# A planner that counts engine exclusion, and matmul operands at one place modulo 512 bytes, in a hybrid encoder block

## The chip, the cores and the metric

The kernel runs as one program on one core of a Trainium2 chip. The metric is device microseconds from a run of the program; before the change it is 2054.53 us, the median of three runs (2053.8 to 2062.17 us). Engines are named as in the profile: PE multiplies matrices (PEld is its weight load), DVE and POOL do elementwise work, ACT does activations and copies, SP issues DMAs.

## The reference

The block is one layer over a sequence of 1024 frames of width 1024, in float32. Two mixers run on the projected input and are gated and summed; then come an output projection and a convolutional feed-forward network, each with a residual and a layer norm.

```python
proj = h @ w_in                               # h: (1024, 1024), w_in: (1024, 7456)
u, v, rk, gates = split(proj)
y_a = gelu(u) * (blockwise w_s @ layer_norm(gelu(v)) + b_s)
rk = rk + (token_shift(rk) - rk) * mu_shift
r, k, val, wd, ad, gd = split(rk)
y_b = rwkv7(r, k, val, decay(wd), a(ad), gate(gd))   # 16 heads of 64, a recurrence over the frames
m = sigmoid(gate_a) * y_a + sigmoid(gate_b) * y_b
x = layer_norm(alpha * h + m @ w_o)
g, val = split(x @ w_up)                      # 2 x 2688 columns
x = layer_norm(alpha * x + (gelu(conv3(g)) * val) @ w_down)
```

## The kernel before, in words

Every large product is kept accurate in three passes: each operand is split into a high part rounded to fp32r and a low remainder, and `mm3` issues high by high, high by low and low by high into one PSUM bank. One such matmul has a 128x128 stationary operand and 512 moving columns. These "wide" matmuls are the bulk of PE's work.

The program has five stretches:

- Layer norm of the trunk input, transposition into `xh`/`xlo`, and the value projection `v` of the gating unit (tiles `vh`, `vl`, `pv`).
- The interleaved stretch. `load_w` fetches a 512 KB weight tile `wr` over SP, ACT rounds it to `wh`, POOL subtracts to get `wl`; `gemm` multiplies it with `xh`/`xlo` into `ps` (47 such tiles, 48 wide matmuls each). Beside that, 16 units (8 pairs of heads, two halves of the sequence) go through the recurrence: `stage_a` makes `ar`, `bk`, `nb`, `bkt`, `sv` on DVE, ACT and POOL and multiplies `bk` by `ar` into `pp`; `stage_b` solves a triangular system on POOL in 31 steps (`tm`, `yd`); `stage_chain` carries the state through eight chunks (`pc`, `py`, `xs`, `sv`), each chunk waiting for the one before; `stage_fin` finishes the unit.
- The output projection `po`, with `mh`/`ml` (tiles `wh`, `wl`) stationary and `woh`/`wol` moving, and the layer norm after it.
- The feed-forward network in seven groups of three column blocks: up projections `pu` and `ps` (stationary `fuh`/`ful` or `wh`/`wl`, moving `x1h`/`x1l`), convolution and gelu, and down projections `pd` (stationary `th`/`tl`, moving `fdh`/`fdl`), added into `acc` on DVE.
- The final layer norm (`finish`), row block by row block.

In the interleaved stretch the order on each engine is not the order of the Python code. The class `Weave` records every operation, gives it a cost by `cost` (L107 of the code before), links dependent operations, and then `order` (L209) simulates the five engines: it takes whichever engine can start first, and on it the ready operation with the lowest priority number. The order so found is then issued as it stands. PE, DVE, ACT and POOL each run their own list in that order, so an operation that waits holds up everything behind it on its engine. The planner's costs reach the chip only through this order. Outside the interleaved stretch the framework places the operations, and it lets the work of later code slip in between: the last projection weight (rows of L92) stands among the chunks of the last unit's chain.

`tiny` (L280) is a pool of small tiles that lies ahead of nearly everything else in on-chip memory; `gb` (L1043) is a buffer of the convolution, ahead of `t0`, `th` and `tl`.

Of the kernel before, what the change touches and what calls it, by code (L numbers as in the profile page):

```python
# [8 lines left out]
F32 = mybir.dt.float32  # L9
# [5 lines left out]
P = 128  # L15
D = 1024
S = 1024
# [33 lines left out]


class Op:
    __slots__ = ("key", "op", "call", "prio", "cost", "lat", "table", "deps", "users", "left", "ready", "seq", "out", "at", "cls", "wide")


class WovenPool:
# [17 lines left out]
class Weave:  # L75
# [14 lines left out]
    def add(self, key, op, fn, a, k):  # L90
        if not self.on:
            return fn(*a, **k)  # L92
        aps = [q for q in (*a, *k.values()) if isinstance(q, bass.AP)]
        o = Op()
        o.key, o.op, o.call, o.prio = key, op, (fn, a, k), self.prio
        if callable(o.prio):
            o.prio = o.prio(key)
        o.out, o.cls = aps[0], self.cls
        o.table = next((self.TABLE[q] for q in a if isinstance(q, AF) and q in self.TABLE), None) if key == "A" else None
        o.cost, o.lat = self.cost(key, op, aps, a)  # L100
        o.lat += self.late
        o.wide = key == "T" and aps[1].dtype == F32R and aps[0].shape[-1] == HT
        o.deps, o.users, o.seq = set(), [], len(self.ops)
        self.ops.append((o, aps[:1], aps[1:]))

    @staticmethod
    def cost(key, op, aps, a):  # L107
        n = int(np.prod(aps[0].shape[1:]))
        if op == "dma_start":
            return 60, 2000 + aps[0].size() * 4 / 150  # L110
        if key == "T":
            if aps[1].dtype == F32R:
                c = 233 * n / 512
            elif aps[1].shape[0] == 32:
                c = 50
            else:
                c = (1 if op == "transpose" else 2) * max(85 if n <= 64 else 111, 0.87 * n)
            return max(c, 30), 200
        if key == "A":
            return 150 + 0.95 * n, 80  # L120
        if key == "V":
            src = int(np.prod(aps[1].shape[1:])) if len(aps) > 1 else n
            k = max(n, src)
            if op in ("tensor_copy", "tensor_scalar", "tensor_scalar_max", "memset", "reciprocal"):
                return 150 + 0.8 * k, 80
            if op == "transpose":
                return 435, 80
            if op == "tensor_tensor_scan":
                return 190 + 1.7 * k, 80
            return 190 + (1.05 if k < 512 else 1.3) * k, 80  # L130
        if op == "memset":
            return 80 + 0.9 * n, 80
        return (200 + n if op == "tensor_copy" else 230 + 2.15 * n), 80

    @staticmethod
    def cells(ap):
# [71 lines left out]

    def order(self):  # L209
        free = dict.fromkeys("TVAGS", 0.0)  # L210
        held, small = {}, 0.0
        self.held = held
        table, todo = None, {k: [] for k in "TVAGS"}
        for o, _, _ in self.ops:
            o.left, o.ready = len(o.deps), 0.0
            if not o.left:
                todo[o.key].append(o)
        out = []
        while any(todo.values()):
            best = None  # L220
            for k, lst in todo.items():
                if lst:
                    t = max(free[k], min(self.start(o) for o in lst))
                    if best is None or t < best[0]:
                        best = t, k
            t, k = best
            can = [o for o in todo[k] if self.start(o) <= t]
            o = min(can, key=lambda o: (o.prio, o.seq))
            if k == "T":
                wide = [q for q in can if q.wide]  # L230
                if small > 900 and wide and o.cls != "stage_chain":
                    o = min(wide, key=lambda o: (o.prio, o.seq))
                small = 0.0 if o.wide else small + o.cost
            todo[k].remove(o)
            c = o.cost
            if k == "A" and o.table and (table or "-") not in o.table:
                table, c = o.table[0], c + 1283
            o.at = t
            free[k] = t + c
            for name in {ap.tensor.name for ap in self.aps[o.seq]}:  # L240
                if name in self.tag:
                    if name not in held:
                        held[name] = 0.0
                        self.lines[self.line[name]].pop(0)
                        self.next.remove(name)
                        self.room[self.tag[name]].remove(min(self.room[self.tag[name]]))
                    held[name] = max(held[name], t + c + 100)
                    self.uses[name] -= 1
                    if not self.uses[name]:
                        self.room[self.tag[name]].append(held[name])  # L250
            out.append(o)
            for u in o.users:
                u.left -= 1
                u.ready = max(u.ready, t + c + (o.lat if u.key != k or o.op == "dma_start" else 0))
                if not u.left:
                    todo[u.key].append(u)
        assert len(out) == len(self.ops)
        return out
# [13 lines left out]
def hybrid_block(ctx: ExitStack, tc, x, w_in, w_v, pars, rows, bs, ws, lor, w_o, w_up, w_dn, out):  # L272
# [4 lines left out]

    const = ctx.enter_context(tc.tile_pool(name="const", bufs=1))
    dram = ctx.enter_context(tc.tile_pool(name="dram", bufs=1, space=bass.MemoryType.DRAM))
    tiny = W.enter(ctx, tc.tile_pool(name="tiny", bufs=4), 4)  # L280

    v_d = dram.tile([KT, P, KT, P], F32, name="v_d")
    m_d = dram.tile([KT, P, S], F32, name="m_d")
# [710 lines left out]
    with ExitStack() as st:  # L994
# [40 lines left out]
        for g in range(NF // GRP):  # L1035
            hh, hl, wd = [], [], []
            for f in range(g * GRP, (g + 1) * GRP):
                wg = load2(w_up[f], "fu", 2) if f else wg0
                wv = load_w(0, w_up[NF + f]) if f else wv0
                wd.append(load2(w_dn[f * P:(f + 1) * P, :], "fd", GRP))  # L1040
                th = hp.tile([P, S], F32R, name="th")
                tl = hp.tile([P, S], F32R, name="tl")
                gb = fs.tile([P, S + 2], F32, name="gb", bufs=1)  # L1043
                G.memset(gb[:, 0:2], 0.0)
                cw = lambda i: par[:, C_CW + i * NF + f:C_CW + i * NF + f + 1]
                ts = []
                for h in range(2):
                    pg = up(wg, h, True) if f or h else up0[0]
                    A.copy(gb[:, 2 + h * HT:2 + (h + 1) * HT], pg)
                    t0 = fs.tile([P, HT], F32, name="t0", bufs=3)  # L1050
                    A.activation(t0, pg, AF.Identity, bias=par[:, C_CB + f:C_CB + f + 1], scale=cw(2))
                    V.scalar_tensor_tensor(t0, gb[:, 1 + h * HT:1 + (h + 1) * HT], cw(1), t0, ALU.mult, ALU.add)
                    V.scalar_tensor_tensor(t0, gb[:, h * HT:(h + 1) * HT], cw(0), t0, ALU.mult, ALU.add)
                    A.activation(t0, t0, AF.Gelu)
                    ts.append(t0)
                for h in range(2):
                    hs = slice(h * HT, (h + 1) * HT)
                    pv = up(wv, h) if f or h else up0[1]
                    V.tensor_tensor(ts[h], ts[h], pv, ALU.mult)
                    V.tensor_copy(th[:, hs], ts[h])  # L1060
                    G.tensor_tensor(tl[:, hs], ts[h], th[:, hs].bitcast(F32), ALU.subtract)
                hh.append(th)
                hl.append(tl)
            if g == 0:
                bc = load_bc(2)
                for i in range(2):
                    A.mul(bc[i], bc[i], ALPHA)
                for n in range(KT):
                    V.tensor_tensor(acc[n], acc[n], bc[0], ALU.mult)
                    (V if n % 2 else G).tensor_tensor(acc[n], acc[n], bc[1], ALU.add)  # L1070
            if g == NF // GRP - 1:
                bc = load_bc(4)
            for n in range(KT):
                ns = slice(n * P, (n + 1) * P)
                for j in range(2):
                    js = slice(j * HT, (j + 1) * HT)
                    po = ps_d.tile([P, HT], F32, name="pd")
                    for i in range(GRP):
                        mm3(po, hh[i][:, ns], hl[i][:, ns], wd[i][0][:, js], wd[i][1][:, js], i == 0, i == GRP - 1)
                    V.tensor_tensor(acc[n][:, js], acc[n][:, js], po, ALU.add)  # L1080
                if g == NF // GRP - 1:
                    finish(n, bc)
# [65 lines left out]
```

## Time and profile before

| | |
|---|---|
| runs | 2053.8, 2054.53, 2062.17 us |
| profiled execution: own time, span | 2061.35 us, 2059.6 us |
| mean granted PE clock in it | 0.954 of full speed |
| busy share of the span | PE 94%, PEld 75%, DVE 50%, POOL 44%, ACT 41% |
| stretches (us from the span's start) | first 0 to 110, interleaved 110 to 1204, output projection 1204 to 1397, feed-forward 1397 to 2026, end 2026 to 2059.6 |

A matmul's own duration in the profile overlaps its neighbours, so PE's pace is read from start to start, or from the chain of waits, where a row gives the time that a run of matmuls takes and their count. A row of waits names who waited for whom and how long in total. An idle engine costs nothing unless the chain goes through it. [...]

### The profile page before, as it was taken

How to read it: one execution, taken by the hardware profiler on the slowest of the kernel's cores; microseconds unless marked ns; L12 is line 12 of the kernel's file. 1: busy time of each engine (PE TensorE's matmuls, PEld its weight loads, DVE VectorE, ACT ScalarE, POOL GpSimd, SP SyncE). 2: the span in 40 equal slices, each digit the busy share in tenths (PEclk: the TensorE clock that was granted, in tenths of full speed). 3: DMA queues.
4: the chain of work that ended last, by engine and by line, in shares of the span. 5: the costliest groups of instructions: out<-in, count | busy, mean ns of one | idle time of the engine just before them, and what ended most of it. 6: DMA issues, size and time to landing. Idle time of an engine off the chain costs nothing.

```text
span 2059.6 us, 27150 instructions
## 1 busy us (share of the span) xinstructions
PE 1926.8 (94%) x10024; PEld 1541.6 (75%) x10024; DVE 1025.1 (50%) x1786; ACT 852.7 (41%) x1711; POOL 907.6 (44%) x1481
## 2 busy tenths in 40 slices
PE   6997998999999999999998876999999999999997
PEld 5995776667777777777776655877888888888886
DVE  8424545666666555565555257575232323232327
ACT  5443454565555656556654452331212121213121
POOL 5103463556667555556545336073414132323224
PEclk9998898999999999989987888999999999999999
DMA  5111211111111212111111050131112020211102
GB/s 202 45 36 55 56 50 54 50 47 50 47 50 61 63 50 67 41 50 49 53 52 39 25 202 27 39 123 61 62 31 71 22 72 23 70 32 60 42 0 82
DMA packets 76580, 119.13 MB, mean 58 GB/s; under 512 B 27520, under 2 KB 47232, under 8 KB 76448
## 3 DMA queue, kind: packets, MB, share of 16 engines
q1 hardware_dynamic: 59488, 96.94, 15.6%
q10 hardware_dynamic: 16960, 20.45, 3.0%
q8 instruction: 80, 1.31, 0.3%
q14 instruction: 52, 0.43, 0.1%
HBM read 103.08 MB, written 14.29 MB: 57 GB/s over the span
## 4 chain that ended last, share of the span: by engine, by line
PE 40%; DVE 5%; POOL 2%; issue 1%; DMA 1%; ACT 1%; SPq 0%; POOLq 0%; ACTq 0%; DVEq 0%
PE ps L92 11%; PE pd L92 10%; PE pu L92 10%; PE po L92 4%; DVE acc L92 3%; PE ps L267 2%; PE pp L267 2%; PE pc L267 1%; POOL yd L267 1%; POOL tm L267 1%; DVE ln_st L92 0%; PE pt L92 0%; DMA wor<-in_dram 0%; DVE t L92 0%; DVE wl L92 0%
## 5 line engine op out<-in xcount | busy, mean ns | idle before, releaser
L267 PE MATMUL ps<-xh,wh 128*128 128x512 f32 x752 | 323.0, 430 | 23.3 <-ACT wh L267 10.6
L267 PE MATMUL ps<-xh,wl 128*128 128x512 f32 x752 | 319.2, 425 | 4.5 <-POOL wl L267 4.4
L267 PE MATMUL ps<-xlo,wh 128*128 128x512 f32 x752 | 321.1, 427 | 0.0
L92 DVE SCALAR_TENSOR_TENSOR t<-gb,par,t 128x512 f32<-128x512 f32 x84 | 88.5, 1053 | 199.0 <-ACT t L92 197.6
L267 PEld LDWEIGHTS ps<-xh,wh 128*128 128x128 f32 x752 | 147.7, 197 | 51.7 <-ACT wh L267 10.8
L267 POOL TENSOR_TENSOR tm<-yd,da 128x60 f32<-128x60 f32 (+24 forms) x496 | 158.1, 319 | 54.2 <-ACT xs L267 8.7
L267 POOL TENSOR_TENSOR yd<-yd,tm 128x60 f32<-128x60 f32 (+24 forms) x496 | 163.6, 330 | 36.8 <-POOL tm L267 0.2
L267 PEld LDWEIGHTS ps<-xh,wl 128*128 128x128 f32 x752 | 147.3, 196 | 32.1 <-POOL wl L267 6.1
L267 DVE SCALAR_TENSOR_TENSOR sv<-pc,gam,sgm 64x64 f32<-64x64 f32 x240 | 68.0, 283 | 199.0 <-PE pc L267 197.0
L267 POOL TENSOR_TENSOR wl<-wr,wh 128x1024 fp32r<-128x1024 f32 x47 | 116.4, 2477 | 114.6 <-ACT wh L267 73.3
L267 PEld LDWEIGHTS ps<-xlo,wh 128*128 128x128 f32 x752 | 147.8, 197 | 25.0 <-issue 2.3
L92 DVE TENSOR_TENSOR acc<-acc,pd 128x512 f32<-128x512 f32 x112 | 76.8, 686 | 134.0 <-PE pd L92 133.9
L92 POOL TENSOR_TENSOR fdl<-wr,fdh 128x1024 fp32r<-128x1024 f32 x21 | 52.5, 2512 | 204.2 <-ACT fdh L92 204.2
L92 PE MATMUL ps<-x1h,wh 128*128 128x512 f32 x344 | 137.0, 398 | 3.3 <-DVE t L92 3.3
L92 PE MATMUL ps<-x1l,wh 128*128 128x512 f32 x344 | 136.7, 397 | 0.0
L92 PE MATMUL ps<-x1h,wl 128*128 128x512 f32 x344 | 136.6, 397 | 0.0
L92 PE MATMUL pd<-fdh,tl 128*128 128x512 f32 x336 | 132.9, 396 | 0.0
L92 PE MATMUL pd<-fdh,th 128*128 128x512 f32 x336 | 132.9, 395 | 0.0
L92 PE MATMUL pd<-fdl,th 128*128 128x512 f32 x336 | 132.9, 395 | 0.0
L92 PE MATMUL pu<-x1h,fuh 128*128 128x512 f32 x320 | 126.2, 395 | 0.4 <-ACT t L92 0.4
L92 PE MATMUL pu<-x1h,ful 128*128 128x512 f32 x320 | 126.2, 394 | 0.0
L92 PE MATMUL pu<-x1l,fuh 128*128 128x512 f32 x320 | 126.2, 394 | 0.0
(249 smaller groups left out, 4336.5 us busy)
## 6 DMA issues: line engine op xcount, KB each, us to landing
wr<-in_dram SPq DMA_DIRECT2D x113, 512.0 KB
da<-a_d SPq DMA_DIRECT2D x64, 128.0 KB
vraw<-in_dram SPq DMA_DIRECT2D x8, 528.0 KB
xt<-in_dram SPq DMA_DIRECT2D x8, 512.0 KB
v_d<-xt ACTq DMA_DIRECT2D x8, 512.0 KB
fv<-v_d ACTq DMA_DIRECT2D x16, 256.0 KB
f<-q_d SPq DMA_DIRECT2D x32, 128.0 KB
wor<-in_dram SPq DMA_DIRECT2D x8, 512.0 KB
```

What stands on the lines that cost most here:

```text
L92: return fn(*a, **k)
L267: fn(*a, **k)
```

## The change

It has two parts.

The planner. Costs are set anew: an ACT operation costs 150 + 0.85 per element, plus 100 for every per-partition operand; a DVE copy is cheaper when both sides are in SBUF; a two-operand DVE operation is 165 + 1.02 per element; POOL's tensor_tensor is 190 + 2.12 per element. A new test `port` marks two-operand operations of at least 256 elements: all of POOL's, and those of DVE whose two inputs both lie in SBUF. `order` lets only one marked operation run at a time: a marked one is lengthened until the marked one before it has ended.

The layout. `tiny` keeps 3 buffers of each of its ten tiles and not 4, and `gb` is 128 columns wider than the sequence and not 2. Both shift what lies behind them. In the built program the places of the matmul operands modulo 512 bytes become:

```
operands (stationary by moving)                 before        after
projections   wh, wl   by xh, xlo               288 by 480    480 by 480
output        wh, wl   by woh, wol              288 by 288    480 by 480
up            fuh, ful, wh, wl by x1h, x1l      288 by 480    480 by 480
down          th, tl   by fdh, fdl              320 by 288    480 by 480
values        xh, xlo  by vh, vl                480 by 64 to 448 in steps of 128    480 by 0 to 384 in steps of 128
```

```diff
+        o.port = key in "VG" and self.port(key, op, aps)
...
         if key == "A":
-            return 150 + 0.95 * n, 80
+            return 150 + 0.85 * n + 100 * (sum(q.shape[1] == 1 for q in aps[2:])), 80
...
-                return 150 + 0.8 * k, 80
+                return 150 + (0.65 if all(sb) else 1.02) * k, 80
...
-            return 190 + (1.05 if k < 512 else 1.3) * k, 80
+            return 165 + 1.02 * k + (50 if op == "scalar_tensor_tensor" and not all(sb) else 0), 80
...
-        return (200 + n if op == "tensor_copy" else 230 + 2.15 * n), 80
+        return (280 + n if op == "tensor_copy" else 190 + 2.12 * n if n > 256 else 190 + 1.9 * n), 80
+
+    @staticmethod
+    def port(key, op, aps):
+        n = int(np.prod(aps[0].shape[1:]))
+        if n < 256 or op not in ("tensor_tensor", "scalar_tensor_tensor"):
+            return False
+        two = [q for q in aps[1:] if q.space == bass.MemoryType.SB and int(np.prod(q.shape[1:])) > 1]
+        return key == "G" or key == "V" and len(two) > 1
...
-            o.at = t
+            if o.port:
+                c += max(0.0, port - t)
+                port = t + c
+            o.at, o.took = t, c
...
-    tiny = W.enter(ctx, tc.tile_pool(name="tiny", bufs=4), 4)
+    tiny = W.enter(ctx, tc.tile_pool(name="tiny", bufs=3), 3)
...
-                gb = fs.tile([P, S + 2], F32, name="gb", bufs=1)
+                gb = fs.tile([P, S + P], F32, name="gb", bufs=1)
```

The same operations are issued, 8093 of them in the interleaved stretch; only their order on the engines differs. Three places show it. The units are counted from 0 to 15, and L267 before is L279 after.

On POOL, where it makes `ar` of unit 11 (`ar_3093`) beside the remainder `wl_3135` of a projection weight and the solve of unit 10 (`tm`, `yd`), before:

```order
L267 TENSOR_TENSOR tm_3067<-yd_3045,da_3044 128x60
L267 TENSOR_TENSOR yd_3045<-yd_3045,tm_3067 128x6x10
L267 TENSOR_TENSOR ar_3093<-t_r_2841,gam_3091 64x8x64
L267 TENSOR_TENSOR wl_3135<-wr_3133,wh_3134 128x1024
L267 TENSOR_TENSOR ar_3093<-t_r_2841,gam_3091 64x8x64
L267 TENSOR_TENSOR f_3106<-f_3106,f_3090 128x512
```

and after:

```order
L279 TENSOR_TENSOR wl_3135<-wr_3133,wh_3134 128x1024
L279 MEMSET gam_3091 128x8
L279 TENSOR_TENSOR tm_3065<-yd_3045,da_3044 128x60
L279 TENSOR_TENSOR yd_3045<-yd_3045,tm_3065 128x5x12
L279 TENSOR_TENSOR tm_3066<-yd_3045,da_3044 128x66
L279 TENSOR_TENSOR ar_3093<-t_r_2841,gam_3091 64x8x64 x2
L279 TENSOR_TENSOR yd_3045<-yd_3045,tm_3066 128x6x11
```

The weight's remainder has moved ahead of both halves of `ar`, which now follow each other.

On PE, at the first matmuls of unit 11 that read `ar` and `bk`, before:

```order
L267 MATMUL ps_3126<-xlo0_120,wh_3124 128x512
L267 MATMUL ps_3126<-xh0_118,wl_3125 128x512
L267 MATMUL pp_3097<-ar_3093,bk_3094 128x128 x4
L267 MATMUL pp_3098<-ar_3093,bk_3094 128x128 x4
L267 MATMUL ps_3136<-xh0_118,wh_3134 128x512
L267 MATMUL ps_3136<-xlo0_120,wh_3134 128x512
```

and after:

```order
L279 MATMUL ps_3130<-xlo1_121,wh_3124 128x512
L279 MATMUL ps_3130<-xh1_119,wl_3125 128x512
L279 MATMUL ps_3136<-xh0_118,wh_3134 128x512
L279 MATMUL pp_3040<-ident_71,ff_2993 128x128 x4
L279 MATMUL pp_3042<-gd0_136,g0w_2612 128x512
L279 MATMUL pp_3042<-gd1_137,g1w_2614 128x512
L279 MATMUL pp_3097<-ar_3093,bk_3094 128x128 x4
L279 MATMUL pp_3098<-ar_3093,bk_3094 128x128
L279 MATMUL ps_3136<-xlo0_120,wh_3134 128x512
```

The whole second half of that weight's matmuls (`ps_3130`) and the end of the unit before (`pp_3040`, `pp_3042`) now stand ahead of the reading of `ar`. Counted in wide matmuls that stand ahead of it, the reading of `ar` comes 14 to 42 later in units 6 to 15 (25 in unit 11), and -7 to 21 later in units 0 to 5.

On PE, at the last chunks of the last unit's chain, before:

```order
L267 MATMUL pc_3865<-xs_3863,yi1_1496 128x64
L92 MATMUL ps_12053<-xh0_118,wh_12049 128x512
L92 MATMUL ps_12053<-xlo0_120,wh_12049 128x512
L267 MATMUL pc_3866<-sv_3704,bkt_3701 128x128
L267 MATMUL py_3851<-sv_3704,nb_3696 128x128
L92 MATMUL ps_12053<-xh0_118,wl_12050 128x512
L92 MATMUL ps_12082<-xh1_119,wh_12049 128x512
L92 MATMUL ps_12082<-xlo1_121,wh_12049 128x512
```

and after:

```order
L279 MATMUL pc_3865<-xs_3863,yi1_1496 128x64
L279 MATMUL pc_3866<-sv_3704,bkt_3701 128x128
L279 MATMUL py_3851<-sv_3704,nb_3696 128x128
L279 MATMUL pc_3867<-sv_3704,ar_3693 128x128
L279 MATMUL py_3851<-sv_3704,ar_3693 128x128
L279 MATMUL pc_3870<-xs_3868,yi1_1496 128x64
L279 MATMUL pc_3871<-sv_3704,bkt_3701 128x128
L279 MATMUL py_3851<-sv_3704,nb_3696 128x128
```

The wide matmuls that stood between the last chunks have moved ahead. From the first chunk of the last unit's chain (its first `pc<-xs`) to the first `po`, 80 wide matmuls stood beside and behind the chain before, and 42 do now.

## Rows read from the trace of the kernel before

**Rows 1.** Busy time and granted clock by stretch, one row for each stretch.

```profile
core 0: us, PE busy (x) PEld busy (x) DVE busy (x) ACT busy (x) POOL busy (x), PEclk, DMA share, GB/s
110.00:1204.00 1094.00, 1018.60 (x6015) 803.34 (x6014) 595.04 (x1170) 591.71 (x1316) 570.85 (x1252) 0.93 0.17 50
1204.00:1397.00 193.00, 164.10 (x691) 129.30 (x690) 137.05 (x145) 69.67 (x121) 96.19 (x39) 0.93 0.32 104
1397.00:2026.00 629.00, 629.00 (x2686) 505.17 (x2687) 195.46 (x265) 126.63 (x170) 184.13 (x112) 1.00 0.15 44
2026.00:2059.60 33.60, 23.20 (x100) 18.35 (x98) 29.60 (x59) 7.51 (x14) 20.03 (x16) 0.88 0.32 118
```

**Rows 2.** Chain that ended last: start, us, what; runs of wide matmuls without waits.

```profile
1304.33 10.90 PE po L92 x48
...
1612.46 33.59 PE pd L92 x144
1646.05 11.20 PE pu L92 x48
1657.25 11.20 PE ps L92 x48
```

**Rows 3.** Timeline of PE, interleaved stretch: start us, us, what; clock granted in full.

```profile
1142.37 0.39 PE L267 MATMUL ps<-xh,wl 128*128 128x512 f32 x1
1142.61 0.40 PE L267 MATMUL ps<-xh,wh 128*128 128x512 f32 x1
1142.84 0.39 PE L267 MATMUL ps<-xlo,wh 128*128 128x512 f32 x1
```

**Rows 4.** Groups of PE, interleaved stretch: count | busy us, mean ns | idle before.

```profile
L267 PE MATMUL ps<-xh,wh 128*128 128x512 f32 x752 | 323.0, 430 | 23.3 <-ACT wh L267 10.6 <-ACT gu L267 3.9 <-DVE t_r L267 3.0
L267 PE MATMUL pp<-ar,bk 64*128 64x128 f32 x512 | 92.9, 337 | 26.4 <-DVE ar L267 14.0 <-POOL yd L267 5.9 <-POOL sh L267 4.9
```

**Rows 5.** Timeline of POOL at unit 11.

```profile
829.06 1.69 POOL L267 TENSOR_TENSOR ar<-t_r,gam 64x512 f32<-64x512 f32 x1
830.72 2.38 POOL L267 TENSOR_TENSOR wl<-wr,wh 128x1024 fp32r<-128x1024 f32 x1
833.18 1.52 POOL L267 TENSOR_TENSOR ar<-t_r,gam 64x512 f32<-64x512 f32 x1
```

**Rows 6.** Timeline of DVE at the same place.

```profile
829.02 4.63 DVE L267 SCALAR_TENSOR_TENSOR f<-f 128x512 f32<-128x512 f32 x2 [1.48 <-ACT gam L267]
835.17 0.68 DVE L267 TENSOR_TENSOR f<-f,t_k 128x512 f32<-128x512 f32 x1
```

**Rows 7.** Timeline of PE at the same place.

```profile
834.10 0.40 PE L267 MATMUL ps<-xh,wl 128*128 128x512 f32 x1
838.38 0.34 PE L267 MATMUL pp<-ar,bk 64*128 64x128 f32 x1 [3.89 <-DVE ar L267]
```

**Rows 8.** Timeline of PE with the clock at half speed.

```profile
1162.26 0.63 PE L267 MATMUL ps<-xlo,wh 128*128 128x512 f32 x1
1162.69 0.63 PE L267 MATMUL ps<-xh,wl 128*128 128x512 f32 x1
```

**Rows 9.** Timeline of PE: first and last chunk of the last unit's chain.

```profile
1170.38 0.43 PE L267 MATMUL pc<-xs,yi 128*128 128x64 f32 x2
...
1196.14 0.43 PE L267 MATMUL pc<-xs,yi 128*128 128x64 f32 x2 [0.17 <-ACT xs L267]
```

**Rows 10.** Chain from 1360 to 1397 us, shares by line.

```profile
by line: DVE acc L92 63.0%; DVE t L92 20.3%; issue 8.7%; PE ps L92 8.4%; DVE th L92 0.1%
```

**Rows 11.** Chain at the end of the interleaved stretch, and in the final layer norm.

```profile
1202.62 1.77 PE pp L267 x7
...
1206.28 8.15 DMA wor<-in_dram
...
2036.01 1.09 DVE acc L92
...
2040.42 1.10 DVE acc L92
...
2044.83 1.10 DVE acc L92
```

More of the change, by code (lines that the diff above doesn't have):

```diff
@@ L53 @@
 class Op:
-    __slots__ = ("key", "op", "call", "prio", "cost", "lat", "table", "deps", "users", "left", "ready", "seq", "out", "at", "cls", "wide")
+    __slots__ = ("key", "op", "call", "prio", "cost", "lat", "table", "deps", "users", "left", "ready", "seq", "out", "at", "cls", "wide", "port", "took")
 class WovenPool:
@@ L119, in cost @@
         if key == "A":
-            return 150 + 0.95 * n, 80
+            return 150 + 0.85 * n + 100 * (sum(q.shape[1] == 1 for q in aps[2:])), 80
+        sb = [q.space == bass.MemoryType.SB for q in aps]
         if key == "V":
-            src = int(np.prod(aps[1].shape[1:])) if len(aps) > 1 else n
-            k = max(n, src)
+            k = max(n, int(np.prod(aps[1].shape[1:])) if len(aps) > 1 else n)
             if op in ("tensor_copy", "tensor_scalar", "tensor_scalar_max", "memset", "reciprocal"):
-                return 150 + 0.8 * k, 80
+                return 150 + (0.65 if all(sb) else 1.02) * k, 80
             if op == "transpose":
@@ L210, in order @@
         free = dict.fromkeys("TVAGS", 0.0)
-        held, small = {}, 0.0
+        held, small, port = {}, 0.0, 0.0
         self.held = held
```

## The prediction

> **What bounds the kernel now.** I read the busy times by stretch first [rows 1]. PE is busy 1018.6 of 1094 us in the interleaved stretch and all of the 629 us of the feed-forward stretch, where no other engine passes a third; together these are 84% of the span. So the time is PE's pace in the second, and PE's pace plus its waits in the first. Only two short stretches are bounded otherwise: the output projection, where PE idles 29 of 193 us and much of the chain from 1360 to 1397 us is DVE on `acc` and `t` [rows 10], and the final layer norm, whose steps come every 4.41 us on DVE (2040.42 - 2036.01 [rows 11]) while its 18 wide matmuls need 4.2.
>
> Then I read the pace itself, from the chain [rows 2], because there a run of wide matmuls follows without waits. Up and down projections take 11.20 us for 48 and 33.59 us for 144: 233.3 ns each. The output projection takes 10.90 us for 48: 227.1 ns. The shape, the number of passes, the clock and the engine are the same. The interleaved projections also come every 0.23 to 0.24 us (1142.37, 1142.61, 1142.84 [rows 3]). What sets the output projection apart, in the table of places, is that stationary and moving operand lie at one place modulo 512 bytes. Where the matmuls take longer, the places differ by 192 bytes (up, projections) or by only 32 (down), and both cost the same 6 ns, so it looks like equal or not equal, and not like a distance.
>
> **The change, part by part.**
>
> Layout in the feed-forward stretch. All up and down operands come to 480. I take 227.1 ns for them, the nearest row there is. The stretch has 2686 wide matmuls [rows 1] at 233.3, with nothing that PE waits for that matters; 2686 x 6.2 = 16.7 us less. DVE (195 of 629 us), ACT and POOL have room for a pace 2.7% faster. The bound on the other side is 0, if the 6 ns have another cause. Ahead of 1397 the first groups gain at most 1.5 us (some 250 such matmuls) and I count 0, since DVE bounds that piece [rows 10]; the final layer norm gains 0 for the same reason [rows 11].
>
> [...] The rows above show 233.3 beside 227.1. [...] No run so far moves an address alone.
>
> Layout in the interleaved stretch. 3 x 752 = 2256 wide projections [rows 4] at up to 6.2 ns make 14.0 us at most, 0 at least. Where the wide matmuls fill the time of a PE that is never idle, all of it counts; where PE waits for the chain or for DVE and POOL, the wait ends when it did. PE is idle 75 of 1094 us and at reduced clock for a part of the rest (0.93 [rows 1]), so most counts. I take two thirds, 9 us.
>
> Layout elsewhere. The output projection is equal before and after (288 by 288, then 480 by 480). The value projection is unequal in both, so I put 0. Small matmuls of the recurrence have both operands in pools that move together; 0.
>
> `tiny` with 3 buffers. A statistic waits for the reader of the one three calls back instead of four. Those readers are a few short steps on the same engines, long done when the next statistic of that tag is written: 0. The wider `gb` costs addresses only.
>
> The planner's order. Its aim can be seen at unit 11. POOL runs `ar`, `wl`, `ar` back to back from 829.06 to 834.70 [rows 5]. In the same time DVE's two operations on `f` take 4.63 us, where an operation of that size takes 0.68 us a little later [rows 6]; so they stood still for some 3.3 us while POOL ran. `ar` came late by that, and PE waited 3.89 us for it [rows 7]. The old costs did not know of this. The new order puts 25 more wide matmuls, 25 x 0.233 = 5.8 us, ahead of that reading, which is more than the wait. The same holds in all late units (14 to 42 more). PE waited 26.4 us in total ahead of the `ar` by `bk` matmuls [rows 4]. All of it gone is the upper end. It will not all go, since DVE and POOL still exclude each other as much and `ar` is no earlier for being read later; also the end of the unit before (`pp<-ident,ff`) now stands ahead of it and can wait instead. I take half, 13.2 us.
>
> Against it stands the end. The last unit's chain, whose seven steps from first to last chunk took 25.8 us, 3.7 each [rows 9], has 38 fewer wide matmuls beside and behind it (80 to 42). If the chunks come at the same pace, PE stands idle there for what these were worth: 38 x 0.233 = 8.9 us; it is 0 if the chunks come closer together once nothing stands between them. Behind the chain waits `stage_fin`, and behind that the load of the output weights, 8.15 us [rows 11], which no order shortens. I count the whole 8.9. The order so gives 13.2 - 8.9 = 4.3 us less; ends: 26.4 less, 8.9 more.
>
> **Sum.** 16.7 + 9.0 + 4.3 = 30.0 us less. From the profiled execution's own 2061.35 us that is 2031.4. That execution lies at the upper end of the three runs shown (2053.8 to 2062.17), so from their median, 2054.53, I forecast 2024.5 us, 1.5% less.
>
> **Rivals.**
>
> Only the feed-forward stretch gains. The interleaved stretch is then bound by its dependences (the chunks of the chain, the solves on POOL, the loads behind one `wr` buffer), a quicker PE waits longer, and the order gives and takes alike. For it: the waits there are spread over ACT, DVE and POOL and none is large, so removing some may uncover others. Against it: PE is 93% busy there. Time: 2054.5 - 16.7 = 2037.8.
>
> [...]
>
> The order does harm, and more than the layout gives. Place: the ends of the late units' chains, where the wide matmuls that moved ahead are missing. [...] The stretch has now 7% of its clock missing, about 150 us at half clock. Time at half clock costs half of itself. To end above the time before, the layout's 25.7 us must be eaten: 8.9 at the end, and another 17 that need 34 us more at half clock, a granted clock of 0.91 or less. With twice that, 66 us more and a granted clock of 0.90, the time is about 2054.5 - 25.7 + 8.9 + 33 = 2070.7. [...] Against it: the chains of units 0 to 14 have other projections beside them.
>
> **How the numbers follow.** Forecast (both layout terms, order a little better) 0.52; only the feed-forward 0.28; address without effect 0.13; order does harm 0.07. About 0.5%, 10 us, is what a measurement of this kernel can tell from no change: faster than 2044.3 is all of the first, nearly all of the second and a fifth of the third: 0.82. Within 0.5%: most of the third and a part of the fourth, 0.13. Slower: 0.05. The range goes from 2004 (16.7, the full 14.0 and 20 us of the order's 26.4) to 2046 (the second rival with the order's 8.9 us against it, 2046.7).
>
> **What would show it.** In the profile of the changed kernel the runs of 48 up projections should take 10.9 us instead of 11.20, of 144 down projections 32.7 instead of 33.59, and the feed-forward stretch should last some 612 us. If they stay at 11.20, the layout term is wrong. Projections in the interleaved stretch should come 0.227 us apart. The wait ahead of `ar` by `bk` should fall from 26.4 us to about 13, with the two operations on `f` at unit 11 no longer spread over 4.63 us beside POOL's `wl`; if another wait on the same stretch grows by as much, the order's term is wrong. The time from the last chain's start to the first `po` should not grow. The interleaved stretch as a whole should be some 13 us shorter; the prediction is wrong if it is longer.

## The result, and the profile after

| | before | after |
|---|---|---|
| median of 4 runs on one chip | 2057.02 us (2053.8 to 2062.17) | 1979.96 us (1979.24 to 1981.83) |
| ratio | | 0.9625, interval 0.9601 to 0.9648 |
| profiled execution, its span | 2061.35, 2059.6 us | 1981.83, 1980.1 us |
| mean granted PE clock | 0.954 | 0.972 |

The time fell by 77 us. The forecast was 30 (2024.5 us), its range ended at 2004. The sign and the feed-forward term were right, the size was not.

The view by stretch of the changed kernel stands beside [rows 1]. Columns: stretch, length, busy us of PE, PEld, DVE, ACT and POOL, granted clock, DMA share, GB/s.

```profile
110.00:1142.00 1032.00, 978.28 (x6012) 766.73 (x6010) 587.51 (x1171) 580.96 (x1308) 569.21 (x1252) 0.97 0.18 54
1142.00:1336.00 194.00, 163.29 (x691) 129.17 (x691) 136.78 (x144) 67.59 (x119) 94.79 (x39) 0.90 0.31 101
1336.00:1948.00 612.00, 612.00 (x2693) 506.48 (x2693) 197.93 (x268) 127.08 (x171) 185.42 (x113) 1.00 0.15 45
1948.00:1980.00 32.00, 20.88 (x93) 16.95 (x91) 28.12 (x56) 7.21 (x13) 18.60 (x14) 0.86 0.33 123
```

The interleaved stretch went from 1094 to 1032 us, the feed-forward stretch from 629 to 612, the rest stayed. In the interleaved stretch two columns moved: PE's idle time (length less busy) from 75.4 to 53.7 us, and the granted clock from 0.93 to 0.97.

The chain of the changed kernel, as in [rows 2], shows the layout's part:

```profile
1219.16 10.91 PE po L92 x48
...
1446.64 32.64 PE pd L92 x144
1479.28 10.88 PE pu L92 x48
1490.16 10.88 PE ps L92 x48
```

Up and down projections come every 226.7 ns (10.88 / 48, 32.64 / 144), as the output projection did before.

The groups of PE in the interleaved stretch, as in [rows 4]:

```profile
L279 PE MATMUL ps<-xh,wh 128*128 128x512 f32 x752 | 314.7, 418 | 21.7 <-ACT wh L279 10.3 <-DVE t_k L279 6.0 <-DVE t_r L279 4.5
L279 PE MATMUL pp<-ar,bk 64*128 64x128 f32 x512 | 74.8, 288 | 2.5 <-ACT ff L279 2.4
L279 PE MATMUL pp<-x,nb 32*32 32x32 f32 x512 | 11.4, 195 | 10.4 <-DVE x L279 9.4 <-ACT sv L279 0.9
```

The 26.4 us ahead of `ar` by `bk` are down to 2.5, and none of it is a wait for `ar` to speak of. Some came back ahead of `x` by `nb` in `stage_b` (10.4, before 1.8).

For a finer account I took the stretch from 110 us to the last `pp<-gd,g1w`, about the interleaved stretch, and split it into PE's idle time, half of the time in which PE worked at half clock (that half is the loss: at half clock a wide matmul came every 0.43 us [rows 8] and at full clock every 0.233; the trace records each fall and rise of the clock, here between 1.0 and 0.5 of full speed), and the rest, which is work at full clock.

| kernel | length | PE idle | half-clock loss | rest |
|---|---|---|---|---|
| before | 1093.6 | 75.4 | 62.6 | 955.6 |
| after | 1031.9 | 53.7 | 20.9 | 957.3 |
| layout alone | 1094.4 | 79.5 | 66.1 | 948.7 |
| order alone | 1039.1 | 53.7 | 22.0 | 963.5 |
| costs and layout, no exclusion | 1101.8 | 76.6 | 83.5 | 941.7 |
| exclusion and layout, old costs | 1109.2 | 92.6 | 62.9 | 953.8 |
| before, waits filled | 1059.9 | 53.1 | 23.9 | 982.9 |
| after, waits put in | 1092.7 | 74.6 | 59.8 | 958.4 |
| after, `acc` on DVE | 1040.9 | 56.1 | 28.6 | 956.3 |
| the same, waits filled | 1024.3 | 41.9 | 12.5 | 969.9 |

The matmuls in it are the same throughout, but for 100 and 88 throwaway ones in the two filled kernels, two small ones for each wait put in, and 30 fewer wide ones of later code with costs only. From before to after 21.7 us of idling went, and 41.7 us of half-clock loss. The forecast has nothing for the second. The theory from here on (A in the first expectations, D in the later ones): a wait of PE costs itself and, behind it, microseconds at half clock. The rival: the layout does more in the interleaved stretch than its 6 ns.

### The profile page after: what moved, and what is told of

Read it like the earlier page. It is cut to its first block, busy times and chain, and to the rows that moved or that the text cites. A ratio compares the mean times of both kernels' runs of the same rounds, so it can differ in the third digit from the quotient of the medians.

```text
span 1980.1 us, 27146 instructions
## 1 busy us (share of the span) xinstructions
PE 1865.9 (94%) x10024; PEld 1504.3 (76%) x10024; DVE 1018.3 (51%) x1786; ACT 840.0 (42%) x1701; POOL 905.2 (46%) x1481
## 4 chain that ended last, share of the span: by engine, by line
PE 72%; POOL 10%; DVE 9%; issue 3%; DMA 3%; ACT 2%; ACTq 0%; SPq 0%; POOLq 0%; DVEq 0%
PE ps L279 18%; PE ps L92 12%; PE pu L92 10%; PE pd L92 10%; PE pp L279 8%; PE po L92 4%; POOL yd L279 4%; POOL tm L279 4%; PE pv L92 4%; PE pc L279 3%; DVE acc L92 3%; PE py L279 2%; POOL wl L279 1%; DVE ln_st L92 1%; POOL ar L279 1%
## 5 line engine op out<-in xcount | busy, mean ns | idle before, releaser
L279 PE MATMUL ps<-xh,wh 128*128 128x512 f32 x752 | 314.7, 418 | 21.7 <-ACT wh L279 10.3
L279 PE MATMUL ps<-xh,wl 128*128 128x512 f32 x752 | 311.2, 414 | 4.2 <-POOL wl L279 4.2
L279 PE MATMUL ps<-xlo,wh 128*128 128x512 f32 x752 | 312.7, 416 | 0.0
L279 POOL TENSOR_TENSOR tm<-yd,da 128x60 f32<-128x60 f32 (+24 forms) x496 | 161.6, 326 | 81.3 <-DMA da<-a_d 19.3
L279 POOL TENSOR_TENSOR yd<-yd,tm 128x60 f32<-128x60 f32 (+24 forms) x496 | 167.1, 337 | 37.3
L279 PEld LDWEIGHTS ps<-xh,wh 128*128 128x128 f32 x752 | 144.9, 193 | 46.1 <-ACT wh L279 10.5
L279 PEld LDWEIGHTS ps<-xh,wl 128*128 128x128 f32 x752 | 144.5, 192 | 29.9 <-POOL wl L279 5.6
L279 PEld LDWEIGHTS ps<-xlo,wh 128*128 128x128 f32 x752 | 145.0, 193 | 23.8 <-issue 0.7
L279 POOL TENSOR_TENSOR wl<-wr,wh 128x1024 fp32r<-128x1024 f32 x47 | 115.4, 2456 | 100.4 <-ACT wh L279 79.8
L279 DVE SCALAR_TENSOR_TENSOR sv<-pc,gam,sgm 64x64 f32<-64x64 f32 x240 | 67.8, 282 | 150.7 <-PE pc L279 148.7
```

## Experiments

Ratios are to the kernel before on the same chip.

**Layout alone.** Of the two numbers in the line, the first is the pool's own count of buffers, the second the count that the planner reckons with; it stays at 4, so that the order stays.

```diff
-    tiny = W.enter(ctx, tc.tile_pool(name="tiny", bufs=4), 4)
+    tiny = W.enter(ctx, tc.tile_pool(name="tiny", bufs=3), 4)
-                gb = fs.tile([P, S + 2], F32, name="gb", bufs=1)
+                gb = fs.tile([P, S + P], F32, name="gb", bufs=1)
```

> The kernel before with its order on every engine, and the operand places of the changed kernel (480 by 480). Theory A (each PE wait that the new order removes also cost the microseconds at half clock behind it; the layout gives about 6 ns per wide matmul and no more): the feed-forward stretch shortens by 17 us, the interleaved stretch by 0 to 14, the waits for `ar` by `bk` and the half-clock stretches behind them stay; 2026 to 2040 us. Rival B (the layout alone brought the 61 us of the interleaved stretch, because PE's loads and reads no longer collide there): 1975 to 2000 us, and the half-clock stretches go with the order unchanged. Rival C (the places do nothing): 2057 us.

2042.2 us, ratio 0.9919 (0.9887 to 0.9951): 14.7 us less, just outside theory A's range. The window of the interleaved stretch is where it was:

```profile
110.00:1204.00 1094.00, 1014.46 (x6009) 803.49 (x6008) 599.70 (x1170) 590.94 (x1315) 570.14 (x1252) 0.93 0.17 50
```

PE's work is shorter (the rest falls by 6.9 us), and in this profile idling and half clock take all of it back (4.1 + 3.5). From the first `pu` to the last `pd` the time falls from 701.4 to 682.5 us, so with before's order the feed-forward stretch is the whole gain that shows. Rival B is out.

**Order alone.** The changed kernel with a pad of 320 bytes ahead of `tiny`'s tiles and `gb` as before.

```diff
+    pad = tiny.tile([P, 80], F32, name="pad", bufs=1)
+    G.memset(pad[:, 0:1], 0.0)
-                gb = fs.tile([P, S + P], F32, name="gb", bufs=1)
+                gb = fs.tile([P, S + 2], F32, name="gb", bufs=1)
```

> The changed kernel's order, with a pad that puts the operands back to the places of before (288 by 480, 320 by 288). Theory A: up and down projections back at 233 ns per matmul, waits for `ar` gone, most half-clock stretches gone; 2003 to 2020 us. Rival B: 2040 to 2057 us.

2002.2 us, ratio 0.9727 (0.9706 to 0.9749): 54.7 us less from the order alone, 0.8 us beyond theory A's range. From the chain, the pace of before is back:

```profile
1352.63 33.59 PE pd L92 x144
1386.22 11.20 PE pu L92 x48
```

The interleaved stretch and its `ar` waits, with the old places, are much as in the changed kernel:

```profile
110.00:1149.00 1039.00, 985.29 (x6014) 769.43 (x6013) 583.03 (x1171) 581.12 (x1308) 569.84 (x1252) 0.97 0.18 53
L279 PE MATMUL pp<-ar,bk 64*128 64x128 f32 x512 | 74.1, 287 | 3.1 <-ACT ff L279 2.1 <-DVE ar L279 1.0
```

On top of the new order the layout is worth 2002.2 - 1980.0 = 22.2 us: some 18 in the feed-forward stretch (from the first `pu` to the last `pd` 700.3 us, then 682.5), and the other 4 ahead of it, where the rest of the account falls by 6.2.

**The planner's two halves.** First the marks of exclusion are left out, costs and layout kept.

```diff
-        o.port = key in "VG" and self.port(key, op, aps)
+        o.port = False
```

> The changed kernel without the exclusion in the planner (no operation is marked), with its new costs and its layout. If the exclusion is the part that removes the waits: the waits for `ar` come back, 2005 to 2030 us. If the new costs alone remove them: 1978 to 1992 us.

2044.72 us, ratio 0.9930 (0.9909 to 0.9952). Groups of PE:

```profile
L279 PE MATMUL pp<-ar,bk 64*128 64x128 f32 x512 | 98.7, 363 | 34.8 <-DVE bk L279 17.7 <-POOL tm L279 6.4 <-DVE ar L279 5.1
L279 PE MATMUL pp<-x,nb 32*32 32x32 f32 x512 | 11.3, 194 | 13.0 <-DVE x L279 13.0
```

Then the exclusion with the old costs (the cost lines of the diff taken back, `port` and the layout kept).

> The changed kernel with the planner's old costs, but with the exclusion, and with its layout. If the exclusion is the part that removes the waits: 1978 to 1995 us. If the new costs do: 2005 to 2030 us, with PE waits for `ar` of 20 us or more.

2055.12 us, ratio 0.9997 (0.9979 to 1.0015). Groups of PE:

```profile
L279 PE MATMUL ps<-xh,wl 128*128 128x512 f32 x752 | 314.7, 419 | 26.2 <-POOL sh L279 19.4 <-POOL wl L279 6.8
L279 PE MATMUL pp<-ar,bk 64*128 64x128 f32 x512 | 74.4, 292 | 4.1 <-DVE ar L279 3.4 <-POOL yd L279 0.6
```

Neither half does it, though both kernels have the 15 to 22 us of the layout. My expectation that one of the two carries the gain is wrong. With the exclusion and the old costs the waits for `ar` nearly all go, waits for POOL ahead of `wl` come instead, and the stretch loses as much to the half clock as before (62.9 us). So the half clock is not tied to the `ar` waits. The length of a wait does not settle it either. By the clock records of this trace, six waits of 2.8 to 3.1 us ahead of `wl` have 31 us at half clock at or behind them, four waits of only 0.81 us among the `ar` by `bk` matmuls of units 8, 10, 12 and 14 have 38 us that begin within 3 us of them, and one wait of 3.48 us, at 201.4 us, has none.

Why it takes both halves stays open. The planner's own reckoning of the stretch, which starts a little later than my account, ends at 895.0 us in the kernel before, 885.6 after, 860.0 with costs only and 970.1 with the exclusion only. The chip takes 199, 146, 242 and 139 us more than that. The miss is smaller with the exclusion, but it is smallest in the kernel with the exclusion only, which gains nothing, so a better reckoning alone is not shown to make fewer waits.

**Waits filled.** The kernel before, with 100 more wide matmuls ahead of the first `ar` by `bk` of six units.

```diff
+FILL = {2: 20, 11: 17, 12: 11, 13: 17, 14: 11, 15: 24}
...
                 fn, a, k = o.call
+                if o.fill:
+                    for _ in range(o.fill[1]):
+                        self.tc.nc.tensor.matmul(o.fill[0], *self.junk, start=True, stop=True)
                 fn(*a, **k)
```

> The kernel before, its order and layout untouched, with 100 wide matmuls more, whose product is thrown away (each writes a `pp` tile that the next real matmuls overwrite): 20, 17, 11, 17, 11 and 24 of them right ahead of the first matmul of `bk` by `ar` of units 2, 11, 12, 13, 14 and 15, where PE waits 2.5 to 5.5 us. Theory D (a wait of PE costs more than itself, because the clock is at half for 7 to 24 us behind it; of 82 us at half clock behind these six waits, half is the loss): 2015 to 2040 us, faster with more work. Rival E (the half clock comes from what stands there, the narrow matmuls, and not from the wait): 2050 to 2062 us. Rival F (the extra matmuls push the work back): 2062 us or more.

2028.03 us, ratio 0.9871 (0.9842 to 0.9899): 29 us less with 100 matmuls more. Windows from the six waits (of units 2, 11, 12, 13, 14 and 15) on, in the kernel before:

```profile
311.00:331.00 20.00, 15.38 (x52) 11.65 (x51) 12.53 (x18) 4.97 (x9) 5.92 (x6) 0.57 0.12 31
834.00:846.00 12.00, 8.11 (x33) 6.50 (x32) 9.95 (x14) 6.73 (x15) 9.03 (x22) 0.73 0.19 51
904.00:921.00 17.00, 14.54 (x50) 10.94 (x49) 11.12 (x18) 5.14 (x10) 5.18 (x5) 0.61 0.16 40
964.00:976.00 12.00, 8.12 (x30) 6.62 (x29) 10.36 (x15) 7.05 (x15) 9.19 (x20) 0.72 0.18 51
1034.00:1051.00 17.00, 14.54 (x48) 11.04 (x47) 11.22 (x18) 5.04 (x9) 5.74 (x5) 0.60 0.18 45
1092.00:1116.00 24.00, 17.11 (x57) 12.87 (x57) 16.34 (x25) 10.14 (x19) 12.02 (x16) 0.50 0.12 29
```

and at the places of units 11 and 15 with the fill:

```profile
825.00:837.00 12.00, 12.00 (x60) 9.32 (x58) 11.67 (x17) 9.44 (x18) 9.30 (x18) 1.00 0.18 50
1067.00:1091.00 24.00, 22.13 (x177) 17.35 (x175) 17.71 (x31) 12.00 (x23) 13.43 (x17) 0.96 0.25 72
```

The 24 us at half clock from the start of unit 15's wait on, 5.5 of them the wait itself, are at 0.96 now. In the account, 22.3 us of idling turn into work (the rest grows by 27.3), and 38.7 us of half-clock loss go; the two profiled executions lie 38 us apart, more than the 29 of the medians. Theory D holds for these six waits. F falls, and so does E as the whole cause: the same narrow matmuls still stand there.

**Waits put in.** The reverse: the changed kernel, with PE made to wait for a DMA ahead of the same matmul of six other units.

```diff
+STALL = (4, 6, 8, 10, 12, 14)
...
+                    nc.tensor.matmul(o.stall, stat, pad, start=True, stop=True)
+                    nc.sync.dma_start(pad, src)
+                    nc.tensor.matmul(o.stall, stat, pad, start=True, stop=True)
                 fn(*a, **k)
```

> The changed kernel with six PE waits put in, ahead of the first matmul of `bk` by `ar` of units 4, 6, 8, 10, 12 and 14, where it has none: a small matmul reads a scratch tile, SP reloads the tile with a DMA of 32 KB, a second small matmul reads it again. The scratch tile shifts the operand places to 224 by 480, 256 bytes apart. With the changed kernel at 1980 to 1988 us at those places and 2 to 2.5 us per wait: theory D (each wait is followed by 3 to 17 us at half clock) 2008 to 2050 us; if a wait costs only itself, 1993 to 2004 us.

2035.09 us, ratio 0.9903 (0.9874 to 0.9933). The group of the second small matmul gives the waits (two instructions for each), and the windows from each wait on show what follows:

```profile
L287 PE MATMUL pp<-jp,ident 128*128 128x64 f32 x12 | 3.6, 398 | 22.4 <-DMA jp<-in_dram 22.4
```

```profile
421.00:440.00 19.00, 17.26 (x70) 13.70 (x69) 8.08 (x16) 6.87 (x14) 2.35 (x1) 0.64 0.17 45
542.00:562.00 20.00, 16.03 (x61) 13.00 (x61) 9.16 (x14) 6.04 (x11) 4.67 (x4) 0.57 0.25 67
665.00:686.00 21.00, 15.79 (x65) 12.71 (x64) 5.98 (x12) 5.01 (x11) 3.29 (x5) 0.67 0.16 40
790.00:812.00 22.00, 17.95 (x68) 14.62 (x67) 8.50 (x16) 6.16 (x14) 0.26 (x2) 0.61 0.14 38
920.00:946.00 26.00, 20.30 (x104) 15.92 (x103) 11.38 (x17) 7.70 (x15) 3.40 (x4) 0.61 0.12 32
1058.00:1066.00 8.00, 6.24 (x30) 4.82 (x28) 3.64 (x7) 2.47 (x5) 0.00 (x0) 0.82 0.06 11
```

Six waits of 22.4 us together cost 55 us against the changed kernel (47 against its single run at the same operand places, below). A window's length times twice the missing clock is its time at half clock: 19 x 2 x 0.36 = 13.7 us at the first, 17.1, 13.7, 17.1 and 20.5 at the next four, by the clock records, and 3.4 at the last. Against the changed kernel, idling grows by 20.9 us in the account and the half-clock loss by 38.9. Four of the six waits were longer than the 2 to 2.5 us that I had counted (up to 5.7), and the half clock behind them, 3.4 to 20.5 us, is about the 3 to 17 of theory D.

**Places 64 and 128 bytes apart, and 256.** The changed kernel's order, a pad of 64 or 256 bytes, and `gb` narrower by 96 or 64 columns.

> The changed kernel's order with the operand places 64 bytes apart modulo 512 for projections, output and up projections (32 by 480), 128 apart for down projections (160 by 32). If only equal places are fast: 233 ns per matmul in both, about 1998 us. If places within 64 or 128 bytes are still good: 227 in the one or the other.

> The same with places 256 bytes apart for all (224 by 480, 480 by 224). If what counts is the place modulo 512: 233 ns, about 2000 us. If it is the place modulo 256 or less: 227 ns, about 1982 us.

Single runs of 2003.44 and 1987.57 us. The chain of the first (up projections 64 apart, down 128):

```profile
1353.74 33.46 PE pd L92 x144
1387.20 11.20 PE pu L92 x48
```

and of the second (256 apart for both):

```profile
1387.12 10.88 PE pu L92 x48
...
1452.40 32.64 PE pd L92 x144
```

64 apart costs 233.3 ns, 128 apart 232.4, and 256 apart 226.7, the same as equal places. So, of the distances tried, only multiples of 256 are quick; "modulo 512" asks for more than is needed. The expectations are wrong on the output projection: its operands lie at equal places in both built programs (32 by 32 and 224 by 224), and 48 of its matmuls take 10.90 to 10.93 us in both.

**What is left in the changed kernel.** The largest single wait of PE after is in the output projection, 15.15 us. Timeline of all engines there:

```profile
1184.82 21.22 POOL L92 TENSOR_TENSOR acc<-acc,wor 128x1024 f32<-128x1024 f32 x8
...
1190.55 2.56 DVE L92 CAST x1h<-xf 128x512 fp32r<-128x512 f32 x1
...
1193.14 2.71 DVE L92 TENSOR_TENSOR x1l<-xf,x1h 128x512 fp32r<-128x512 f32 x1
1195.79 2.56 DVE L92 CAST x1h<-xf 128x512 fp32r<-128x512 f32 x1
...
1201.01 2.82 DVE L92 TENSOR_SCALAR acc<-acc,ln_mv,rs_r 128x1024 f32<-128x1024 f32 x1
...
1203.89 1.97 PE L92 MATMUL pt<-ident,acc 128*128 128x128 f32 x8 [15.15 <-DVE acc L92]
```

Each of these DVE operations takes about as long as one of POOL's (21.22 / 8 = 2.65 us), whether it has 512 columns or 1024. The planner has no say here, since the stretch lies outside it. So `acc` goes to DVE:

```diff
-            G.tensor_tensor(acc[n], acc[n], bx[0], ALU.mult)
-            G.tensor_tensor(acc[n], acc[n], bx[1], ALU.add)
+            V.tensor_tensor(acc[n], acc[n], bx[0], ALU.mult)
+            V.tensor_tensor(acc[n], acc[n], bx[1], ALU.add)
```

> The changed kernel with the 16 full-width operations `acc` by `wor` of the output projection on DVE in place of POOL. If POOL's 41 us run of them is what stretches DVE's casts and subtractions there from 0.4 to 0.7 us to 2.6 to 2.7 (one DVE operation per POOL operation) and so makes PE wait 15.2 us at 1188.4 us: the wait falls under 4 us, the 17 us at half clock behind it go, 1956 to 1970 us. If DVE's own 16 us more are no better: 1978 to 1990 us.

1965.25 us, ratio 0.9553 (0.9528 to 0.9578). Groups of DVE and PE in it:

```profile
L92 DVE TENSOR_TENSOR acc<-acc,wor 128x1024 f32<-128x1024 f32 x16 | 19.1, 1208 | 0.0
L92 DVE CAST x1h<-xf 128x512 fp32r<-128x512 f32 x16 | 6.8, 423 | 11.6 <-ACT xf L92 11.4
L92 PE MATMUL pt<-ident,acc 128*128 128x128 f32 x64 | 8.6, 277 | 0.8 <-DVE acc L92 0.8
```

PE's 16.0 us ahead of `pt` (13.4 in the kernel before) are 0.8, and DVE spends 19.1 us on what took POOL 41.0. The same kernel with throwaway matmuls where the interleaved stretch still waits:

> The kernel of the run before this one, and throwaway matmuls where PE still waits in the interleaved stretch: 21, 14, 15 and 28 of 256 columns ahead of the first matmul of `x` by `nb` of units 0, 1, 13 and 15, and 10 of 512 columns ahead of the transposes of `ff` of the last unit. Theory D (half clock follows a wait): 4 to 12 us under that kernel. Rival F (the extra work delays): equal or up to 5 us above it.

1952.18 us, ratio 0.9491 (0.9468 to 0.9514), 13 us less again, slightly more than expected. This is the best version, 28 us under the change. A caution: with one and the same order the half-clock time of the interleaved stretch was 58 us in the profile after, 62 with the order alone, 71 at 256 bytes and 77 with `acc` on DVE, so half-clock losses of single profiles can differ by some 9 us by chance.

## Why the prediction was wrong

**The planner's order: the step that failed.** The step reads "I take half, 13.2 us", less 8.9 for the end, 4.3 in sum. The order alone gave 54.7. The account from before to the order alone: idling 21.7 less, half-clock loss 40.6 less, rest 7.9 more (most of it in the narrow matmuls: waits and half clock taken off, they come every 84 ns instead of 82, which I did not follow up), 54.4 in sum.

- The waits. All but 2.5 of the 26.4 us went (all but 3.1 with the order alone) where I counted on half. My reason for half was that `ar` is no earlier for being read later, but PE needs `ar` only when it gets there. At unit 11 after (timeline of all engines):

```profile
800.06 3.56 DVE L279 SCALAR_TENSOR_TENSOR f<-f 128x512 f32<-128x512 f32 x2 [0.51 <-ACT gam L279]
800.22 2.85 POOL L279 TENSOR_TENSOR wl<-wr,wh 128x1024 fp32r<-128x1024 f32 x1
804.95 3.24 POOL L279 TENSOR_TENSOR ar<-t_r,gam 64x512 f32<-64x512 f32 x2
808.44 0.60 PE L279 MATMUL pp<-ident,ff 128*128 128x128 f32 x4
810.06 1.16 PE L279 MATMUL pp<-ar,bk 64*128 64x128 f32 x8
```

The two operations on `f` still stand beside POOL's `wl` for 3.56 us (4.63 in [rows 6]; I had said that they would not). The exclusion is as it was; what changed is that PE comes after it. The fear that other waits grow was half right: `x` by `nb` took 8.6 us.

- The half clock. It was in the profile, and in my working only as a price of harm: "Time at half clock costs half of itself" stands in the rival. I never asked what the 150 us at half clock that I read from [rows 1] came from. Six of the falls of the clock in the kernel before stand directly at the `ar` waits, of units 2 and 11 to 15, with 82 us at half clock in and behind them; PE worked in 73 of these. Had I priced those six at 22.8 us of waiting (their rows in the trace) plus half of the 73, the order's term would have been 59, or 50 after the 8.9 for the end. The two experiments with waits filled and put in show that this is cause and effect, in both directions. They do not give a price for any wait: in the kernel before, one of 2.35 us at 717.8 us has no half clock behind it.

- The end of the last chain. I counted 8.9 us of new idling. Timeline of PE, first and last chunk and first `po`:

```profile
1109.62 0.33 PE L279 MATMUL pc<-xs,yi 128*128 128x64 f32 x2
...
1133.19 0.69 PE L279 MATMUL pc<-xs,yi 128*128 128x64 f32 x2 [0.19 <-ACT xs L279]
...
1144.15 1.19 PE L92 MATMUL po<-woh,wh 128*128 128x512 f32 x2 [0.87 <-DVE yb L279]
```

Seven steps take 23.6 us instead of 25.8 [rows 9], and from the first chunk to the first `po` it is 34.5 instead of 37.0. The chunks came closer together, the end of the bound that I did not take.

**Layout in the feed-forward stretch: right.** 226.7 ns where I took 227.1, and 612 us as forecast. "Equal or not equal" was too narrow: 256 bytes apart are as quick. An address without effect, which had 0.13 of my chances, is out: with the order untouched, places 64 bytes apart and not equal moved a run of 48 up projections from 10.88 us to 11.20.

**Layout in the interleaved stretch: 9.0 less forecast; 0.8 more and 7.2 less measured.** Beside the old order the waits and the half clock grew by what the matmuls lost (1093.6 and 1094.4 us in the account); beside the new one 7.2 us stay (1039.1 and 1031.9). That the order makes the difference is not shown, since single profiles differ by as much. The rival "only the feed-forward stretch gains" fits the layout alone.

**`tiny` with 3 buffers: right**, as far as PE's waits tell: none on a statistic's buffer is among its groups after.

## What to carry to other kernels

Price a PE wait in a matmul-bound stretch with the clock behind it: read the granted clock in the microseconds after each wait before deciding what removing it is worth (here from nothing to some 20 us at half clock), and where the wait can't be removed, try throwaway matmuls in it. Put stationary and moving operands at one place modulo 256 bytes; it costs a pad and was worth 2.8% of a run of fp32r matmuls of 512 columns here (233.3 to 226.7 ns each). An order computed from costs has to be judged on the chip as a whole: here each half of the new model gave nothing, and both together 55 us.

## What the hardware showed

- The pace of a wide matmul follows the distance of the operands' places: 226.7 ns at 0 and 256 apart, 232.4 to 233.3 at 32, 64, 128 and 192.
- A wait of 1.7 us (up to 423.8 us, waits put in; one of 1.5 us for `wl` ended 5.6 us before) was followed by 13.7 us at half clock, another of 1.8 us by 3.4, four of 0.81 us by 6.8 to 13.7 (exclusion with old costs), and one of 3.48 us by none. What else decides it stays open.
- DVE's cast and its tensor_scalar with one full input were stretched beside POOL's operations on `acc`, like the two-input subtraction there: the cast took 2.56 us, the tensor_scalar 2.82 and the subtraction `x1l` 2.71, and with `acc` on DVE 0.42 (mean), 0.80 (at best) and 0.68 (mean). The planner's new `port` marks two-input operations only.
